# Gathered expert rows in a decoder block: arithmetic one step behind the gather, another rank and another pace in the dense pass

## The chip, the cores and the metric

The kernel runs on one core of a Trainium2 chip. The metric is device time in microseconds, the median of several runs. The engines are TensorE (PE in the profile, with its weight loads as PEld), VectorE (DVE), ScalarE (ACT), GpSimd (POOL) and SyncE (SP); each works through its own instructions in a fixed order, and waits for the others by semaphores.

## The reference, cut to what matters

One decoder block on 1024 tokens of width 1024: stick-breaking attention and a gated DeltaNet side by side, merged by gates, and then a feed-forward part that fetches single experts. All tensors are float32. The change touches the last part alone:

```python
def peer_ffn(h, w_q, keys1, keys2, u_tab, v_tab):
    q = einsum(h, w_q)                        # 8 heads, two halves of 128
    s1, s2 = q1 @ keys1.T, q2 @ keys2.T       # 128 scores each
    v1, i1 = top_k(s1, 16); v2, i2 = top_k(s2, 16)
    vals, c = top_k(v1[:, None] + v2[None], 16)
    expert = e1 * 128 + e2                    # 16384 experts
    gate = softmax(vals)
    # per block of 128 tokens, 8 heads x 16 = 128 experts for each token
    act = gelu(einsum('td,ted->te', h, u_tab[expert]))
    return einsum('te,ted->td', gate * act, v_tab[expert])
```

## The kernel before

The 1024 tokens are two halves of 512. Each half goes through the mixers (projections, attention, DeltaNet), the merge, the output projection, the norm and the routing (`half`). The feed-forward part is then done in two ways, by blocks of 128 tokens.

Blocks 2, 3, 6 and 7 are dense: every expert is computed for every token, and a gate table of zeros and gates is multiplied in. This is the dense pass (`dense`), the last stage of the program, in 128 chunks of 128 experts. In a chunk TensorE computes the scores (`scores`, 24 matmuls of 512 columns, lines 885 and 887) and the values (24 matmuls by `mm3`, lines 72 to 74), VectorE splits the loaded weights into two parts (line 64, tiles `ut` and `d_v`), multiplies the gates in (`weigh`, line 915), and computes the low part of the product after ScalarE has cast the high part (`rest`, line 906, after line 919). Every fourth chunk it adds four finished accumulators to the output (line 974). The weights stream in on SP's queue, 512 KB at a time.

Blocks 0, 1, 4 and 5 are gathered (`gather_rows`): for each of their 128 experts per token POOL fetches one row of 4 KB per token, 512 KB in all (line 1016), first from `peer_u`, then from `peer_v`. VectorE multiplies a `peer_u` row with the token's hidden state and sums it (line 1019, two instructions, the second reads the sum), or adds a `peer_v` row times its activation to the output (line 1021). That makes 4 x 256 = 1024 rows. In between, after 128 rows, the activations go through Gelu and the gates (lines 1007 and 1009), and the tile of the hidden state is replaced by the output's (line 1011); after 256 rows the output is stored (line 1025) and the next block's hidden state is loaded into the same place (line 1001).

The rows lie in the buffers `gb_row0` to `gb_row3`, used in turn; the dense pass adds two more and takes them off the list at its end. A row can be fetched only when the row that had its buffer is multiplied.

When rows are worked in is decided by `gather(phase)`, which the stages of the second half call once in each step. Each call adds `PACE[phase]` to a count of rows due, and as many whole rows are given out. The rows are given out with a number added to the scheduler's rank (`later`). The scheduler orders the instructions of each engine when the program is built; a smaller rank goes first. The row's arithmetic also gets a bond that keeps it behind VectorE's last instruction at that point (`behind`, the `anchor`). A last call without a phase gives out the rows that are left, after the dense pass.

Of the kernel before, what the change touches and what calls it, by code (L numbers as in the profile page):

```python
# [13 lines left out]
OP = mybir.AluOpType  # L14
# [13 lines left out]
CB = 256  # L28
EPS = 1e-6

PACE = dict(sb=2.2, gdn=1.5, logits=2.5, merge=2.5, out=0.5, route=0, table=0.1, dense=5.25)
NEG = -1e30
C_Q, C_K, C_V = 0, 1024, 2048
C_GQ, C_GK, C_GV, C_GZ = 3072, 4096, 5120, 6144
# [4 lines left out]
class Block:  # L39
    def __init__(self, tc, ins, out):  # L40
        self.tc, self.nc, self.i, self.out, self.tok, self.turn = tc, tc.nc, ins, out, 0, 0
        self.rows, self.due, self.delayed = None, 0.0, []


    @contextmanager
# [947 lines left out]
    def gather_rows(self, blks):  # L993

        nc = self.nc
        n = H * 16
        self.row_bufs = [(self.gp, f"gb_row{k}") for k in range(4)]
        turn = 0
        for blk in blks:
            h2 = self.gp.tile([P, D], F32, name="gb_h2", bufs=1)  # L1000
            nc.sync.dma_start(h2, self.h2_d[blk])
            act = self.gp.tile([P, n], F32, name="gb_act")
            ix = self.expert[blk]
            acc = None
            for p in range(2 * n):
                if p == n:
                    self.acts(nc.scalar.activation(act, act, AF.Gelu))
                    self.back_to_exp()
                    nc.vector.tensor_tensor(act, act, self.gate[blk], op=OP.mult)
                    acc = self.gp.tile([P, D], F32, name="gb_h2", bufs=1)  # L1010
                    nc.sync.dma_start(acc, self.x2_d[blk])
                pool, name = self.row_bufs[turn % len(self.row_bufs)]
                turn += 1
                r = pool.tile([P, D], F32, name=name, bufs=1)
                q = p % n
                nc.gpsimd.indirect_dma_start(out=r, out_offset=None, in_=self.i["peer_u" if p < n else "peer_v"][0],  # L1016
                                             in_offset=bass.IndirectOffsetOnAxis(ap=ix[:, q:q + 1], axis=0))
                if p < n:
                    i = nc.vector.scalar_tensor_tensor(r, r, 1.0, h2, op0=OP.mult, op1=OP.mult, accum_out=act[:, q:q + 1])  # L1019
                else:  # L1020
                    i = nc.vector.scalar_tensor_tensor(acc, r, act[:, q:q + 1], acc, op0=OP.mult, op1=OP.add)  # L1021
                if self.anchor is not None:
                    self.behind(i, self.anchor)
                if p == 2 * n - 1:
                    nc.sync.dma_start(self.out[0, blk * P:(blk + 1) * P, :], acc)
                yield

    def last_dve(self):
        ins = self.nc.cur_bb.bb.instructions
        return next(i for i in reversed(ins) if i.engine == mybir.EngineType.DVE)  # L1030
# [14 lines left out]
    def gather(self, phase=None):  # L1045

        if self.rows is None:
            return
        if phase is None:
            self.anchor = None  # L1050
            for _ in self.rows:
                pass
            return
        self.due += PACE[phase]
        self.anchor = self.last_dve()
        with self.later(1000000):
            while self.due >= 1:
                self.due -= 1
                next(self.rows, None)

    def half(self, half, hx, new_h, st, x2_in):

# [35 lines left out]
def block_kernel(tc, ins, out, x2_in=None, dense_blks=(2, 3, 6, 7), G=8):  # L1098
    b = Block(tc, ins, out)
    b.dense_blks = list(dense_blks)  # L1100
    nc = tc.nc
    with ExitStack() as ctx:
# [14 lines left out]
        b.pz = pool(name="pz", bufs=2, space=PSUM)  # L1117
        b.pc = pool(name="pc", bufs=2, space=PSUM)
        b.gp = pool(name="gp", bufs=1)
        gctx = ctx.enter_context(ExitStack())  # L1120
        cg = gctx.enter_context(tc.tile_pool(name="cg", bufs=1, side="right"))
        b.rb = gctx.enter_context(tc.tile_pool(name="rb", bufs=1, side="right"))
# [56 lines left out]
```

## Time and profile before

| | us |
|---|---|
| three runs, median (lowest to highest) | 3876.8 (3871.88 to 3877.51) |
| the profiled execution, its own time | 3877.26 |
| its span, first to last instruction | 3875.4 |
| TensorE busy | 3596.4 (93%) |
| VectorE busy | 3077.5 (79%) |
| ScalarE busy | 1740.7 (45%) |
| POOL busy | 1356.6 (35%) |

The span has these stages, read from the times of their lines: the first half to about 1014 us, when the first row is gathered; the second half's mixers, merge, projection, norm and routing to about 2130 us; the gate tables to about 2384 us; the dense pass to 3853 us; and the last rows to 3872 us. An engine's busy share over the whole span mixes these stages, so the views below are of single stretches.

### The profile page before, as it was taken

Reading aid. Unit: us, or ns where it says so; the run is one execution under the profiler, and the core shown is the slowest. Engines: PE = TensorE matmul, PEld = TensorE weight load, DVE = VectorE, ACT = ScalarE, POOL = GpSimd, SP = SyncE. Lnnn points to the kernel's source line nnn. Section 1 sums busy time; section 2 is a strip of 40 time slices with the busy share of each in tenths; the row PEclk is TensorE's granted clock in tenths of the full one; section 3 lists DMA queues with packets and bytes.
Section 4 is the critical chain, followed back from the end, with each engine's and each line's share of the span. In section 5 each row is a group of like instructions: output and inputs, shape, how many; then the busy total and the mean of one; then the engine's idle time right before and its main releaser. Section 6 shows DMA issues by size and latency. Waiting matters only on the chain.

```text
span 3875.4 us, 53560 instructions
## 1 busy us (share of the span) xinstructions
PE 3596.4 (93%) x18936; PEld 2983.8 (77%) x18936; DVE 3077.5 (79%) x6196; ACT 1740.7 (45%) x3846; POOL 1356.6 (35%) x1034
## 2 busy tenths in 40 slices
PE   8999999999999999998878877999999999999996
PEld 7878888788777688886667666787778787788785
DVE  5345554349988878888879998899898899899898
ACT  6755554333777655553322786222222322222221
POOL 0000000000044332223442003666666665676665
PEclk9999999999999999999989999999999999999998
DMA  4221113553377756558985568999999999999998
GB/s 121 88 82 50 55 50 115 174 186 93 96 256 265 246 191 192 191 182 290 325 307 170 158 185 289 353 361 358 334 365 358 345 371 365 348 364 374 353 359 312
DMA packets 344205, 937.49 MB, mean 242 GB/s; under 512 B 41984, under 2 KB 121088, under 8 KB 339712
## 3 DMA queue, kind: packets, MB, share of 16 engines
q0 software_dynamic: 147456, 536.94, 38.8%
q1 hardware_dynamic: 196480, 397.13, 30.1%
q8 instruction: 149, 2.44, 0.3%
q14 instruction: 120, 0.98, 0.1%
HBM read 864.22 MB, written 69.21 MB: 241 GB/s over the span
## 4 chain that ended last, share of the span: by engine, by line
PE 42%; issue 20%; POOL 12%; DVE 11%; DMA 10%; ACT 4%; SPq 0%; POOLq 0%; DVEq 0%; ACTq 0%
POOL gb_row L1016 12%; PE mm L72 6%; PE mm L74 6%; PE mm L73 6%; DMA gb_row<-peer_v,expert 5%; PE pc L848 3%; DMA gb_row<-peer_u,expert 3%; PE mm L885 2%; PE pz L532 2%; PE pz L526 2%; DVE gb_row L1019 2%; DVE w_lo L64 2%; PE mm L887 1%; PE pc L317 1%; PE pz L295 1%
## 5 line engine op out<-in xcount | busy, mean ns | idle before, releaser
L1016 POOL DMA_INDIRECT gb_row<-peer_u,expert x512 | 693.6, 1355 | 1848.2 <-DVE expert L793 1012.8
L1016 POOL DMA_INDIRECT gb_row<-peer_v,expert x512 | 661.9, 1293 | 656.4 <-DVE gb_h L1021 408.8
L1019 DVE SCALAR_TENSOR_TENSOR gb_row<-gb_row,gb_h 128x1024 f32<-128x1024 f32 x512 | 614.0, 1219 | 133.2 <-DMA gb_row<-peer_u,expert 109.7
L1021 DVE SCALAR_TENSOR_TENSOR gb_h<-gb_row,gb_act,gb_h 128x1024 f32<-128x1024 f32 x512 | 657.7, 1285 | 73.7 <-DMA gb_row<-peer_v,expert 50.4
L885 PE MATMUL mm<-hf,ut 128*128 128x512 f32 x2048 | 491.2, 391 | 6.9 <-DMA hf<-hd 6.9
L919 ACT CAST d_a<-u_act 128x512 fp32r<-128x512 f32 x128 | 79.2, 621 | 926.5 <-DVE u_act L915 917.7
L885 PEld LDWEIGHTS mm<-hf,ut 128*128 128x128 f32 x2048 | 386.1, 189 | 87.7 <-issue 7.6
L64 DVE TENSOR_TENSOR w_lo<-w_raw,w_hi 128x512 fp32r<-128x512 f32 (+1 forms) x450 | 297.6, 682 | 163.9 <-ACT w_hi L63 125.9
L63 ACT CAST w_hi<-w_raw 128x512 fp32r<-128x512 f32 (+1 forms) x450 | 262.1, 620 | 286.2 <-PE mm L73 122.6
L72 PE MATMUL mm<-h,w_hi 128*128 128x512 f32 (+1 forms) x784 | 322.9, 412 | 3.0 <-ACT pj L598 3.0
L74 PE MATMUL mm<-h,w_lo 128*128 128x512 f32 (+1 forms) x784 | 320.6, 409 | 0.0
L73 PE MATMUL mm<-h,w_hi 128*128 128x512 f32 (+1 forms) x784 | 319.7, 408 | 0.0
L72 PE MATMUL pz<-d_v,d_a 128*128 128x512 f32 x680 | 272.8, 401 | 41.2 <-DVE d_acc L974 30.1
L72 PE MATMUL mm<-w_hi,h 128*128 128x256 f32 x1024 | 299.8, 293 | 8.5 <-DVE x L647 5.7
L74 PE MATMUL mm<-w_hi,h 128*128 128x256 f32 x1024 | 294.0, 288 | 4.0 <-DVE h L64 4.0
L73 PE MATMUL mm<-w_lo,h 128*128 128x256 f32 x1024 | 295.1, 288 | 1.0 <-DVE w_lo L64 0.9
L74 PE MATMUL pz<-d_v,d_a 128*128 128x512 f32 x680 | 270.4, 398 | 0.0
L73 PE MATMUL pz<-d_v,d_a 128*128 128x512 f32 x680 | 270.4, 398 | 0.0
L887 PE MATMUL mm<-hf,ut 128*128 128x512 f32 x1024 | 257.0, 391 | 2.5 <-DVE ut L64 2.5
L887 PEld LDWEIGHTS mm<-hf,ut 128*128 128x128 f32 x1024 | 192.8, 188 | 42.8 <-DVE ut L64 3.3
L72 PEld LDWEIGHTS mm<-w_hi,h 128*128 128x128 f32 x1024 | 199.5, 195 | 16.3 <-DVE x L647 6.4
L73 PEld LDWEIGHTS mm<-w_lo,h 128*128 128x128 f32 x1024 | 199.7, 195 | 6.7 <-issue 3.8
(327 smaller groups left out, 7947.9 us busy)
## 6 DMA issues: line engine op xcount, KB each, us to landing
w_raw<-w_in SPq DMA_DIRECT2D x144, 512.0 KB
u_raw<-u_t SPq DMA_DIRECT2D x128, 512.0 KB
v_raw<-v_t SPq DMA_DIRECT2D x128, 512.0 KB
g_d<-gt_stg SPq DMA_DIRECT2D x16, 2048.0 KB
d_g<-g_d SPq DMA_DIRECT2D x31, 1024.0 KB
w_raw<-peer_w_q SPq DMA_DIRECT2D x32, 512.0 KB
gl<-pj SPq DMA_DIRECT2D x32, 256.0 KB
th<-gl SPq DMA_DIRECT2D x32, 256.0 KB
```

The costliest lines, as they stand in the source:

```text
L63: nc.scalar.copy(hi, src)
L64: nc.vector.tensor_tensor(lo, src, hi.bitcast(F32), op=OP.subtract)
L72: mm(out, l[0], r[0], start=first, stop=False)
L73: mm(out, l[0], r[1], start=False, stop=False)
L74: mm(out, l[1], r[0], start=False, stop=last)
L848: self.last_gate = mm(pg[:, u - u0], o2[:, u], o1[:, u], start=True, stop=True)
L885: mm(ps, ut[0][:, k], hx[a][:, k, x0:], start=k + a == 0, stop=False)
L887: mm(ps, ut[1][:, k], hx[0][:, k, x0:], start=False, stop=k == KD - 1)
L919: nc.scalar.copy(hi, act)
L1016: nc.gpsimd.indirect_dma_start(out=r, out_offset=None, in_=self.i["peer_u" if p < n else "peer_v"][0], in_offset=bass.IndirectOffsetOnAxis ...
L1019: i = nc.vector.scalar_tensor_tensor(r, r, 1.0, h2, op0=OP.mult, op1=OP.mult, accum_out=act[:, q:q + 1])
L1021: i = nc.vector.scalar_tensor_tensor(acc, r, act[:, q:q + 1], acc, op0=OP.mult, op1=OP.add)
```

## The change

The pace of the dense pass goes from 5.25 to 5.1 rows per call. A row's gather and its arithmetic are given out apart: `gather_rows` issues the gather and notes what is to be multiplied in a list, `landing`; the new function `multiply` gives the noted multiplications out and empties the list. Ahead of the dense pass `gather` calls `multiply` first, for the rows of the call before, and then gives out the new gathers. In the dense pass `multiply` follows each gather at once, and the rank is 800 instructions on instead of 1000000. Before the Gelu, at the end of a block, and when all buffers are in the list, `multiply` is called too. In the last call, without a phase, each gather is followed by its multiplication.

```diff
-PACE = dict(sb=2.2, gdn=1.5, logits=2.5, merge=2.5, out=0.5, route=0, table=0.1, dense=5.25)
+PACE = dict(sb=2.2, gdn=1.5, logits=2.5, merge=2.5, out=0.5, route=0, table=0.1, dense=5.1)
...
-        self.rows, self.due, self.delayed = None, 0.0, []
+        self.rows, self.due, self.delayed, self.landing = None, 0.0, [], []
...
             for p in range(2 * n):
                 if p == n:
+                    self.multiply()
                     self.acts(nc.scalar.activation(act, act, AF.Gelu))
...
-                if p < n:
-                    i = nc.vector.scalar_tensor_tensor(r, r, 1.0, h2, op0=OP.mult, op1=OP.mult, accum_out=act[:, q:q + 1])
-                else:
-                    i = nc.vector.scalar_tensor_tensor(acc, r, act[:, q:q + 1], acc, op0=OP.mult, op1=OP.add)
-                if self.anchor is not None:
-                    self.behind(i, self.anchor)
+                self.landing.append((p < n, r, h2 if p < n else acc, act[:, q:q + 1]))
                 if p == 2 * n - 1:
+                    self.multiply()
                     nc.sync.dma_start(self.out[0, blk * P:(blk + 1) * P, :], acc)
                 yield
+
+    def multiply(self):
+
+        nc = self.nc
+        for dot, r, x, a in self.landing:
+            if dot:
+                i = nc.vector.scalar_tensor_tensor(r, r, 1.0, x, op0=OP.mult, op1=OP.mult, accum_out=a)
+            else:
+                i = nc.vector.scalar_tensor_tensor(x, r, a, x, op0=OP.mult, op1=OP.add)
+            if self.anchor is not None:
+                self.behind(i, self.anchor)
+        self.landing = []
...
             self.anchor = None
             for _ in self.rows:
-                pass
+                self.multiply()
             return
         self.due += PACE[phase]
         self.anchor = self.last_dve()
-        with self.later(1000000):
+        with self.later(800 if phase == "dense" else 1000000):
+            if phase != "dense":
+                self.multiply()
             while self.due >= 1:
                 self.due -= 1
+                if len(self.landing) == len(self.row_bufs):
+                    self.multiply()
                 next(self.rows, None)
+                if phase == "dense":
+                    self.multiply()
```

Three places show what the change does to VectorE's order. Lines 1019 and 1021 of before are lines 1029 and 1031 after it. Names ending in numbers are single buffers, and their numbers shift by a few between the two programs.

The first place is VectorE in the attention of the second half, ahead of the dense pass; `sb_t`, `sb_a`, `sb_lo` are tiles of the attention. Before:

```order
L300 SCALAR_TENSOR_TENSOR sb_t<-pz_12432,sb_t 128x512
L1019 SCALAR_TENSOR_TENSOR gb_row_11745,gb_act<-gb_row_11745,gb_h_10543 128x1024
L315 TENSOR_TENSOR sb_a<-pz_12377,sb_a 128x384
L64 TENSOR_TENSOR sb_lo<-sb_t,sb_hi 128x512 x2
L1019 SCALAR_TENSOR_TENSOR gb_row_11748,gb_act<-gb_row_11748,gb_h_10543 128x1024
L315 TENSOR_TENSOR sb_a<-pz_12406,sb_a 128x512
```

And now:

```order
L300 SCALAR_TENSOR_TENSOR sb_t<-pz_12430,sb_t 128x512
L1029 SCALAR_TENSOR_TENSOR gb_row_11745,gb_act<-gb_row_11745,gb_h_10543 128x1024
L315 TENSOR_TENSOR sb_a<-pz_12374,sb_a 128x384
L64 TENSOR_TENSOR sb_lo<-sb_t,sb_hi 128x512 x2
L1029 SCALAR_TENSOR_TENSOR gb_row_11747,gb_act<-gb_row_11747,gb_h_10543 128x1024
L315 TENSOR_TENSOR sb_a<-pz_12404,sb_a 128x512
```

Nothing moved: each row's multiplication stands between the same two instructions.

The second place is VectorE in a chunk in the middle of the dense pass, while `peer_v` rows are added. Before:

```order
L1021 SCALAR_TENSOR_TENSOR gb_h_27499<-gb_row_28020,gb_act,gb_h_27499 128x1024
L1021 SCALAR_TENSOR_TENSOR gb_h_27499<-gb_row_28023,gb_act,gb_h_27499 128x1024
L64 TENSOR_TENSOR ut_28065<-u_raw,ut_28064 128x1024
L915 TENSOR_TENSOR u_act<-u_act,d_g 128x512
L1021 SCALAR_TENSOR_TENSOR gb_h_27499<-gb_row_28026,gb_act,gb_h_27499 128x1024
L906 TENSOR_TENSOR d_a_28014<-u_act,d_a_28013 128x512
L1021 SCALAR_TENSOR_TENSOR gb_h_27499<-gb_row_28029,gb_act,gb_h_27499 128x1024
```

And now:

```order
L1031 SCALAR_TENSOR_TENSOR gb_h_27643<-gb_row_28424,gb_act,gb_h_27643 128x1024
L1031 SCALAR_TENSOR_TENSOR gb_h_27643<-gb_row_28427,gb_act,gb_h_27643 128x1024
L64 TENSOR_TENSOR ut_28463<-u_raw,ut_28462 128x1024
L915 TENSOR_TENSOR u_act<-u_act,d_g 128x512
L906 TENSOR_TENSOR d_a_28412<-u_act,d_a_28411 128x512
L1031 SCALAR_TENSOR_TENSOR gb_h_27643<-gb_row_28500,gb_act,gb_h_27643 128x1024
L1031 SCALAR_TENSOR_TENSOR gb_h_27643<-gb_row_28503,gb_act,gb_h_27643 128x1024
```

The row that stood between lines 915 and 906 now stands behind line 906.

The third place is VectorE at the end of the program, from the last two adds of the dense pass on. Before:

```order
L974 TENSOR_TENSOR d_acc<-pz_33397,d_acc 128x512
L974 TENSOR_TENSOR d_acc<-pc,d_acc 128x512
L1021 SCALAR_TENSOR_TENSOR gb_h_31732<-gb_row_33474,gb_act,gb_h_31732 128x1024
L1021 SCALAR_TENSOR_TENSOR gb_h_31732<-gb_row_33477,gb_act,gb_h_31732 128x1024
...
L1021 SCALAR_TENSOR_TENSOR gb_h_31732<-gb_row_33553,gb_act,gb_h_31732 128x1024
L1021 SCALAR_TENSOR_TENSOR gb_h_31732<-gb_row_33556,gb_act,gb_h_31732 128x1024
L1176 UNCONDITIONAL_BRANCH
```

And now:

```order
L974 TENSOR_TENSOR d_acc<-pz_33340,d_acc 128x512
L974 TENSOR_TENSOR d_acc<-pc,d_acc 128x512
L1031 SCALAR_TENSOR_TENSOR gb_h_31942<-gb_row_33420,gb_act,gb_h_31942 128x1024
L1031 SCALAR_TENSOR_TENSOR gb_h_31942<-gb_row_33423,gb_act,gb_h_31942 128x1024
...
L1031 SCALAR_TENSOR_TENSOR gb_h_31942<-gb_row_33561,gb_act,gb_h_31942 128x1024
L1031 SCALAR_TENSOR_TENSOR gb_h_31942<-gb_row_33564,gb_act,gb_h_31942 128x1024
L1191 UNCONDITIONAL_BRANCH
```

Between the last add and the end stand 11 multiplications before and 29 now; 16 of the 29 are those that the last call of `gather` gives out.

## Rows read from the trace of the kernel before

**Rows 1.** Busy time of each engine in two stretches; columns in the first row.

```profile
core 0: us, PE busy (x) PEld busy (x) DVE busy (x) ACT busy (x) POOL busy (x), PEclk, DMA share, GB/s
...
2458.00:3851.00 1393.00, 1341.06 (x5802) 1100.29 (x5802) 1273.49 (x1520) 377.21 (x485) 896.75 (x643) 0.98 0.95 355
3851.00:3876.00 25.00, 0.00 (x0) 0.00 (x0) 16.31 (x15) 0.00 (x0) 7.58 (x7) 0.55 0.76 294
```

**Rows 2.** TensorE's waits in the pass: us, times, longest.

```profile
PE pz L72 <- DVE d_acc L974: 30.1, 14, 4.8
PE pc L72 <- DVE d_acc L974: 18.7, 7, 6.2
```

**Rows 3.** VectorE's waits in the pass, same view.

```profile
DVE gb_row L1019 <- DMA gb_row<-peer_u,expert: 28.5, 30, 2.3
DVE gb_h L1021 <- DMA gb_row<-peer_v,expert: 22.3, 19, 2.1
DVE d_a L906 <- ACT d_a L919: 22.0, 32, 0.7
DVE gb_row L1019 <- DMA gb_h<-h2d: 20.0, 2, 11.5
DVE gb_h L1021 <- DMA gb_h<-x2d: 15.9, 3, 7.7
```

**Rows 4.** VectorE's waits for rows ahead of the pass.

```profile
DVE gb_row L1019 <- DMA gb_row<-peer_u,expert: 65.3, 43, 4.6
DVE gb_h L1021 <- DMA gb_row<-peer_v,expert: 23.9, 21, 3.0
```

**Rows 5.** Multiplications in the pass: count, busy us, mean ns, idle before.

```profile
L1021 DVE SCALAR_TENSOR_TENSOR gb_h<-gb_row,gb_act,gb_h 128x1024 f32<-128x1024 f32 x373 | 479.9, 1287 | 44.6 <-DMA gb_row<-peer_v,expert 22.3 <-DMA gb_h<-x2d 15.9
L1019 DVE SCALAR_TENSOR_TENSOR gb_row<-gb_row,gb_h 128x1024 f32<-128x1024 f32 x271 | 322.2, 1220 | 50.7 <-DMA gb_row<-peer_u,expert 28.5 <-DMA gb_h<-h2d 20.0 <-issue 1.2
```

**Rows 6.** VectorE in order of time, one bubble: start, us, [idle before <- whom].

```profile
3197.86 0.69 DVE L906 TENSOR_TENSOR d_a<-u_act,d_a 128x512 fp32r<-128x512 f32 x1 [0.69 <-ACT d_a L919]
```

**Rows 7.** VectorE in order of time, from 3846 us to the end.

```profile
3846.43 1.29 DVE L1021 SCALAR_TENSOR_TENSOR gb_h<-gb_row,gb_act,gb_h 128x1024 f32<-128x1024 f32 x1 [0.64 <-DMA gb_row<-peer_v,expert]
3848.22 2.66 DVE L1021 SCALAR_TENSOR_TENSOR gb_h<-gb_row,gb_act,gb_h 128x1024 f32<-128x1024 f32 x2 [0.50 <-DMA gb_row<-peer_v,expert]
...
3853.20 6.66 DVE L1021 SCALAR_TENSOR_TENSOR gb_h<-gb_row,gb_act,gb_h 128x1024 f32<-128x1024 f32 x5
3861.58 1.28 DVE L1021 SCALAR_TENSOR_TENSOR gb_h<-gb_row,gb_act,gb_h 128x1024 f32<-128x1024 f32 x1 [1.72 <-DMA gb_row<-peer_v,expert]
3864.10 1.28 DVE L1021 SCALAR_TENSOR_TENSOR gb_h<-gb_row,gb_act,gb_h 128x1024 f32<-128x1024 f32 x1 [1.24 <-DMA gb_row<-peer_v,expert]
3866.61 5.24 DVE L1021 SCALAR_TENSOR_TENSOR gb_h<-gb_row,gb_act,gb_h 128x1024 f32<-128x1024 f32 x4 [1.23 <-DMA gb_row<-peer_v,expert]
```

**Rows 8.** VectorE in order of time, stage with four buffers ahead of the pass.

```profile
1253.97 1.23 DVE L1019 SCALAR_TENSOR_TENSOR gb_row<-gb_row,gb_h 128x1024 f32<-128x1024 f32 x1 [3.40 <-DMA gb_row<-peer_u,expert]
...
1260.65 1.28 DVE L1019 SCALAR_TENSOR_TENSOR gb_row<-gb_row,gb_h 128x1024 f32<-128x1024 f32 x1
...
1270.06 1.22 DVE L1019 SCALAR_TENSOR_TENSOR gb_row<-gb_row,gb_h 128x1024 f32<-128x1024 f32 x1
...
1275.34 1.22 DVE L1019 SCALAR_TENSOR_TENSOR gb_row<-gb_row,gb_h 128x1024 f32<-128x1024 f32 x1 [1.46 <-DMA gb_row<-peer_u,expert]
```

**Rows 9.** POOL in order of time, the same stage.

```profile
1255.48 1.81 POOL L1016 DMA_INDIRECT gb_row<-peer_u,expert  x1 [2.82 <-DVE gb_row L1019]
...
1270.30 1.79 POOL L1016 DMA_INDIRECT gb_row<-peer_u,expert  x1 [2.92 <-DVE gb_row L1019]
```

**Rows 10.** POOL in order of time, the last gathers.

```profile
3840.31 1.01 POOL L1016 DMA_INDIRECT gb_row<-peer_v,expert  x1 [0.30 <-issue]
...
3856.90 1.02 POOL L1016 DMA_INDIRECT gb_row<-peer_v,expert  x1 [0.30 <-issue]
```

More of the change, by code (lines that the diff above doesn't have):

```diff
@@ L996, in gather_rows @@
         n = H * 16
-        self.row_bufs = [(self.gp, f"gb_row{k}") for k in range(4)]
         turn = 0
@@ L1119, in block_kernel @@
         b.gp = pool(name="gp", bufs=1)
+        b.row_bufs = [(b.gp, f"gb_row{k}") for k in range(4)]
         gctx = ctx.enter_context(ExitStack())
```

## The prediction

> **What bounds the kernel now.** I read the stretches first, then the waits of TensorE and VectorE in the dense pass, then VectorE and POOL row by row at the end of the program and in one place ahead of the pass.
>
> [Rows 1] cut out the two stretches that count. From 2458 to 3851 us, the dense pass after its filling, TensorE is busy for 1341.06 of 1393 us, VectorE for 1273.49, and the transfer engines for 95%. From 3851 us on TensorE has nothing left. VectorE alone multiplies the last gathered rows, and the program ends when it is through.
>
> [Rows 2] are TensorE's own waits in the pass: 30.1 + 18.7 = 48.8 us, all for the adds of line 974, with which VectorE empties the accumulators. So VectorE is late there. [Rows 3] say with what. It waits 28.5 + 22.3 = 50.8 us for gathered rows, 20.0 + 15.9 = 35.9 us for the h2 and x2 tiles that change with the token block, and 22.0 us (32 times 0.69) for ScalarE's cast between lines 915 and 906. That is 108.7 of the 119.5 us in which it is idle, and no wait for the accumulators is among them: it always finds them full. The pass therefore goes at VectorE's pace, with TensorE close behind.
>
> **The change part by part.** *Ahead of the pass.* A row's multiplication is now handed to the scheduler one step after its gather. The order of VectorE's instructions, though, is the same as before from the start to the end of the gate tables; POOL's and TensorE's rows are the same to the end. The waits for gathered rows there, 65.3 + 23.9 = 89.2 us [rows 4], are waits of the same instructions in the same places. I cost this part at 0. It would bring something only if the order were not what decides, and I see no way to that. On VectorE nothing is queued differently behind a waiting row, so nothing else can become late.
>
> *In the pass.* The rank of 800 in place of 1000000 and the pace of 5.1 in place of 5.25 both show in the order. Counting rows there: behind VectorE's last add stand 29 multiplications, where 11 stood, so 18 leave the pass. And lines 915 and 906 stand next to each other 53 times, where they did 35 times; the row that stood between them now stands behind.
>
> Relief: 18 multiplications by 1.287 us (the kind that adds into the output, [rows 5]; the other kind has 1.220) are 23.2 us. Against that, 18 more bubbles by 0.69 us [rows 6] are 12.4 us. That leaves 10.8 us. The gathers in the pass fall by 18 of 644, and a buffer is used again a little later; of the 50.8 us of gather waits I let 3 go, an estimate. So the pass becomes 14 us shorter. Bounds: nothing, where TensorE, busy 96% of the time, would itself set the pace, or where the bubbles eat it up; and 48.8 us, since TensorE cannot gain more than it waits for the adds. I stay near the lower half, because 18 instructions carry only 23.2 us and the bubbles are certain.
>
> What hides the removed instructions: nothing, as long as VectorE is the late one. At the two block changes the stores and loads of lines 1025, 1001 and 900 stand in another order on SP's queue, and other instructions stand in front of the row that waits for the new h2: by my estimate 2 us more of work at the first and 4 us less at the second. With [rows 3] at 20.0 us for both waits together that is small, and the gate load now follows the second pair instead of leading it, so I set the two against each other.
>
> *After the pass.* Now 18 rows more are multiplied when TensorE, ScalarE and the weight streams have nothing left to do, so nothing hides them. They run in VectorE's order behind the 11 of before. Those took from 3853.20 to 3871.85 us, 18.65 us [rows 7]: five had their rows already, then three waited for gathers that were on the way together with the output stores.
>
> Sixteen of the rows are now also given out after the two extra buffers are gone (the list is cut back to four at the end of the pass). With four buffers, a row cannot be fetched before the row four places ahead is multiplied. One round is then: from the end of a multiplication 0.28 us until POOL starts (1253.97 + 1.23 = 1255.20, to 1255.48, in the stage with four buffers ahead of the pass, [rows 8, 9]), the time from the gather's start to its row, and the multiplication of 1.28 us. The time from start to row, with gathers and multiplications counted back from the end: the fourteenth from the end, 3840.31 to 3846.43, took 6.12 us, and the fourth, 3856.90 to 3866.61, 9.71 us beside the output stores [rows 7, 10]. Ahead of the pass, 1255.48 to 1260.65 is 5.17 and 1270.30 to 1275.34 is 5.04 us [rows 8, 9]. A round is thus 0.28 + 1.28 + 5.0 to 6.1 = 6.6 to 7.7 us for four rows. The same stage shows four rows in 6.68 us (1253.97 to 1260.65) and in 9.41 us (1260.65 to 1270.06), the second with other work between [rows 8].
>
> Of the 18 rows the first six still find buffers fetched early: 6 by 1.29 = 7.7 us. The other twelve make three rounds of 7.4 us, nearer the upper end, 22.2 us. Together 30 us. Bounds: all 18 at VectorE's own pace, 18 by 1.29 = 23.2 us; and sixteen at 9.41 / 4 = 2.35 us with two at 1.29 us, 40.2 us. I take 30, since the row at 3846.43 us, with the weight streams ended, is the nearest to the new tail.
>
> The Trainium skill, page "DMA: Bandwidth & Descriptors", section "Anatomy of one DMA — SWDGE (gpsimd) path", puts a transfer issued from GpSimd at about 2.0 us plus its bytes by 436 GB/s. For 512 KB that would be an estimate of 3.2 us, and a round of 4.8 us would be shorter than four multiplications, so the buffers would not matter and the sum would be 3886.5 us, as with the first rival below. No row here shows this: the shortest time from a gather's start to its row in the stretches above is 5.04 us.
>
> **The sum.** The profiled execution took 3877.26 us, of which 3875.4 are the span; the median of the runs is 3876.8, so its own time can stand for them. 3877.3 − 14 + 30 = 3893 us.
>
> **The rivals.**
>
> *Gathers land at once in the tail.* If VectorE's pace sets the tail, it costs 23.2 us and the end is 3877.3 − 14 + 23.2 = 3886.5 us. For it: with the streams gone the transfer engines are free. Against it: the 6.12 us from 3840.31 on, when the last weights were long on their way. Chance 0.13.
>
> *The relief pays for the tail.* The pass is saturated on the transfers (95%) and on VectorE, and gathers wait on both. Fewer rows per chunk could take away about half of the 50.8 us of gather waits: a relief of about 10.8 + 20 = 31 us, against a tail of 30, 3876 us. For it: TensorE has 48.8 us to give back, and each wait of VectorE in the pass is handed on to it. Against it: 18 rows of 644 are 3%, little to halve the waits with. Chance 0.15.
>
> *Faster.* The place is the wait for the adds of line 974. If VectorE falls below TensorE's need in most chunks, the lateness built up at a block change is worked off, and all 48.8 us go: 3877.3 − 48.8 + 30 = 3858 us. It decides from a relief of 38 us on, for then the sum is under 3869. For it: VectorE's busy time is already 68 us below TensorE's. Against it: its waits are 108.7 us, and the change does not touch the 35.9 us at the block changes. Chance 0.08.
>
> *No relief.* TensorE is the bound at 96%, the row waits stay, and the bubbles eat the rest: 3877.3 + 30 = 3907 us. Chance 0.04.
>
> That the change does not do what it says is partly the case already, ahead of the pass; it is in the forecast, and it would have to move something that the order does not show to count.
>
> **How the numbers follow.** The forecast, 3893 us, has 0.60. A measurement of this kernel tells about 0.2%, 7.8 us, from no change: faster is below 3869, slower above 3884.6 us. Slower hold the forecast, no relief, and most of the quick gathers, 0.71. Within 0.2% lie the relief that pays for the tail and the remainder of the quick gathers, 0.20. Faster is 0.09. For the range, 14 of relief may be 25, and the tail 23 to 40: from 3876, where the paying relief still is, to 3907, with no more than 2 in 10 outside. The likeliest case's own range is 3885 to 3903.
>
> **What would show it.** In the profile after: the same waits for rows ahead of the pass, near 89 us, and a start of the pass within a few us of before. The last add of line 974 near 3839 us, not 3853. Behind it 29 multiplications in some 48 us, in fours with a wait of 2 to 3 us for a gather ahead of the first. Lines 915 and 906 next to each other with 0.69 us between, some 50 times. I am wrong if the last add comes 30 us earlier or more (the relief), if the waits ahead of the pass shrink (the first part does something), or if the last 18 multiplications follow each other without waits (the tail).

## The result, and the profile after

The kernel after takes 3905.7 us (median of four runs, 3902.9 to 3909.3), the kernel before 3874.7 beside it: a ratio of 1.0080, 95% interval 1.0063 to 1.0098, 31 us slower (24 to 38). The forecast was 16 us slower, in a range that ends at 3907: the measured time lies 1.3 us inside that end, and the loss is nearly twice the one forecast. The profiled execution took 3902.92 us, with a span of 3901.2: 25.8 us more than that of before.

The same stretches as in [rows 1], and ahead of them the filling of the pass, from the end of the gate tables to the first add of line 974 (columns as in [rows 1]). The filling of before:

```profile
2374.00:2458.00 84.00, 71.79 (x322) 57.98 (x322) 59.63 (x89) 31.40 (x47) 41.63 (x30) 0.96 1.00 365
```

The filling, the pass and the end after the change:

```profile
2374.00:2465.00 91.00, 73.99 (x322) 59.50 (x322) 58.91 (x88) 32.10 (x49) 40.56 (x29) 0.94 0.95 342
2465.00:3839.00 1374.00, 1334.17 (x5802) 1095.58 (x5802) 1253.32 (x1502) 372.55 (x483) 888.54 (x625) 0.99 0.95 353
3839.00:3902.00 63.00, 0.00 (x0) 0.00 (x0) 39.88 (x34) 0.00 (x0) 32.29 (x25) 0.53 0.76 266
```

The pass is 18.5 us shorter, the end 37 us longer. The filling, which the prediction left out, is 6.8 us longer. TensorE's waits for the adds, to set against [rows 2], are down from 48.8 to 38.2 us:

```profile
PE pz L72 <- DVE d_acc L974: 28.5, 12, 5.8
PE pc L72 <- DVE d_acc L974: 9.7, 5, 3.7
```

VectorE's waits in the pass, the answer to [rows 3] (us in total, times, longest):

```profile
DVE d_a L906 <- ACT d_a L919: 33.0, 48, 0.7
DVE gb_row L1029 <- DMA gb_row<-peer_u,expert: 24.8, 23, 2.5
DVE gb_row L1029 <- DMA gb_h<-h2d: 18.9, 2, 10.6
DVE gb_h L1031 <- DMA gb_row<-peer_v,expert: 16.9, 11, 3.0
DVE gb_h L1031 <- DMA gb_h<-x2d: 12.4, 3, 5.6
```

The bubbles (the waits of line 906 for ScalarE's cast) cost 11.0 us more, the gathered rows 9.1 less, the block changes 4.6 less; VectorE's busy time fell by 20.2 us. Ahead of the pass the waits for rows are much as in [rows 4], 94.5 us where 89.2 were:

```profile
DVE gb_row L1029 <- DMA gb_row<-peer_u,expert: 70.8, 37, 6.2
DVE gb_h L1031 <- DMA gb_row<-peer_v,expert: 23.7, 21, 3.7
```

VectorE from the last adds on, the answer to [rows 7] (start, duration, count, and in brackets the wait ahead):

```profile
3841.05 0.68 DVE L974 TENSOR_TENSOR d_acc<-pc,d_acc 128x512 f32<-128x512 f32 x1
3841.65 6.55 DVE L1031 SCALAR_TENSOR_TENSOR gb_h<-gb_row,gb_act,gb_h 128x1024 f32<-128x1024 f32 x5
...
3853.85 6.57 DVE L1031 SCALAR_TENSOR_TENSOR gb_h<-gb_row,gb_act,gb_h 128x1024 f32<-128x1024 f32 x5 [0.42 <-DMA gb_row<-peer_v,expert]
3866.00 5.25 DVE L1031 SCALAR_TENSOR_TENSOR gb_h<-gb_row,gb_act,gb_h 128x1024 f32<-128x1024 f32 x4 [5.58 <-DMA gb_row<-peer_v,expert]
3872.74 1.28 DVE L1031 SCALAR_TENSOR_TENSOR gb_h<-gb_row,gb_act,gb_h 128x1024 f32<-128x1024 f32 x1 [1.49 <-DMA gb_row<-peer_v,expert]
...
3884.94 2.67 DVE L1031 SCALAR_TENSOR_TENSOR gb_h<-gb_row,gb_act,gb_h 128x1024 f32<-128x1024 f32 x2 [1.67 <-DMA gb_row<-peer_v,expert]
3888.16 1.28 DVE L1031 SCALAR_TENSOR_TENSOR gb_h<-gb_row,gb_act,gb_h 128x1024 f32<-128x1024 f32 x1 [0.54 <-DMA gb_row<-peer_v,expert]
...
3896.32 1.28 DVE L1031 SCALAR_TENSOR_TENSOR gb_h<-gb_row,gb_act,gb_h 128x1024 f32<-128x1024 f32 x1 [0.98 <-DMA gb_row<-peer_v,expert]
```

The 29 rows take from 3841.65 to 3897.60, 55.95 us; 18.65 + 30 = 48.65 were expected. For the last twelve a round of four takes (3888.16 − 3872.74) / 2 = 7.7 us, and the last one 8.16; 7.4 were forecast. But no wait of 2 to 3 us stands ahead of each four, as was expected: most rows wait by themselves, 0.3 to 1.7 us. What was not forecast is the wait of 5.58 us at 3866.00. POOL's gathers around it, the answer to [rows 10]:

```profile
3855.41 1.86 POOL L1016 DMA_INDIRECT gb_row<-peer_v,expert  x1 [3.00 <-DVE gb_h L1031]
3857.57 1.02 POOL L1016 DMA_INDIRECT gb_row<-peer_v,expert  x1 [0.30 <-issue]
3859.37 1.86 POOL L1016 DMA_INDIRECT gb_row<-peer_v,expert  x1 [0.78 <-DVE gb_h L1031]
```

A gather starts at 3855.41, 10.6 us ahead of the row that waits, but by the numbers of the buffers it is not that row's. VectorE's next multiplication there takes the gather of 3859.37, the third; the first two stand behind it. This gather's row comes 6.6 us after its start. POOL could not start it earlier. Its row is the first one given out after the list of buffers is cut from six to four. By the numbers it gets the buffer of the row multiplied last but one, and the 0.78 us that POOL waits at 3859.37 are for that multiplication.

So I put the order of VectorE's multiplications beside the order of POOL's gathers in the whole program, by the buffers' numbers. Of 1024 multiplications 33 stand at another place than their gather in before, 50 in after; 23 and 34 of these stand in the filling and just behind it, and 3 in the tail of after. In the filling, multiplications 353 to 370 take these gathers (both counted from 0, the gathers along POOL):

```
before 355 356 357 343 359 347 360 358 363 365 361 362 364 366 367 368 369 370
after  357 343 344 358 359 355 360 363 356 366 361 367 362 368 364 370 365 374
```

In after a row that was fetched early is multiplied every second time, and the next one is hardly on its way: 361, 367, 362, 368. The rank is a likely cause, to be tested: with 800 the rows of the pass go ahead of those given out before it, which still have 1000000. VectorE waits for rows in the filling 20.1 us in before and 28.6 us in after (one line of the waits of each):

```profile
DVE gb_row L1019 <- DMA gb_row<-peer_u,expert: 20.1, 12, 5.1
```

```profile
DVE gb_row L1029 <- DMA gb_row<-peer_u,expert: 28.6, 13, 6.6
```

This gave two theories for the 25.8 us: the pace makes all of it (pass and tail), or the rank has a share of its own by the order of rows. And for the tail: four buffers and a gather's way, the transfers beside the output stores, or the order.

### The profile page after: what moved, and what is told of

Its sections match the earlier page's. It is cut to its first block, busy times and chain, and to the rows that moved or that the text cites. A ratio compares the mean times of both kernels' runs of the same rounds, so it can differ in the third digit from the quotient of the medians.

```text
span 3901.2 us, 53527 instructions
## 1 busy us (share of the span) xinstructions
PE 3589.0 (92%) x18936; PEld 2978.7 (76%) x18936; DVE 3079.6 (79%) x6196; ACT 1735.5 (44%) x3846; POOL 1372.6 (35%) x1034
## 4 chain that ended last, share of the span: by engine, by line
PE 36%; issue 25%; POOL 14%; DMA 10%; DVE 10%; ACT 4%; SPq 0%; POOLq 0%; DVEq 0%; ACTq 0%
POOL gb_row L1016 14%; PE mm L72 6%; PE mm L74 6%; PE mm L73 6%; DMA gb_row<-peer_v,expert 5%; PE pc L848 3%; DMA gb_row<-peer_u,expert 2%; PE pz L532 2%; PE pz L526 2%; DVE w_lo L64 1%; DVE gb_row L1029 1%; DVE gb_h L1031 1%; PE pz L522 1%; PE pc L317 1%; PE pz L295 1%
## 5 line engine op out<-in xcount | busy, mean ns | idle before, releaser
L1016 POOL DMA_INDIRECT gb_row<-peer_u,expert x512 | 707.5, 1382 | 1850.8 <-DVE expert L793 1008.9
L72 PEld LDWEIGHTS mm<-w_hi,h 128*128 128x128 f32 x1024 | 200.4, 196 | 18.9 <-DVE x L647 6.9
L74 PEld LDWEIGHTS mm<-w_hi,h 128*128 128x128 f32 x1024 | 200.3, 196 | 7.0 <-DVE h L64 5.2
```

What stands on the lines that cost most here:

```text
L72: mm(out, l[0], r[0], start=first, stop=False)
L74: mm(out, l[1], r[0], start=False, stop=last)
```

## The experiments

Stages of the profiled executions in us, read from starts and ends of lines: *ahead* to the end of the gate tables (line 829), *filling* to the first add of line 974, *pass* to the first of its last four adds, *tail* to the end. So *ahead* ends at 2374 us in before, earlier than the 2384 named for the gate tables above. The last column is the ratio of times to those of before, run beside each kernel, with its 95% interval.

| kernel | ahead | filling | pass | tail | ratio |
|---|---|---|---|---|---|
| before | 2374.1 | 84.3 | 1392.4 | 24.6 | 1 |
| after | 2374.3 | 91.1 | 1373.9 | 61.9 | 1.0080 (1.0063 to 1.0098) |
| pace alone | 2369.3 | 86.6 | 1372.6 | 62.0 | 1.0040 (1.0026 to 1.0055) |
| rank undone | 2381.4 | 84.4 | 1378.9 | 61.7 | 1.0053 (1.0039 to 1.0067) |
| pace undone | 2371.6 | 89.7 | 1401.1 | 24.1 | 1.0043 (1.0027 to 1.0060) |
| pace undone, again | 2375.6 | 90.3 | 1400.0 | 24.0 | 1.0031 (1.0019 to 1.0044) |
| after, in order | 2366.6 | 85.8 | 1378.2 | 60.6 | 1.0056 (1.0038 to 1.0074) |
| before, in order | 2375.0 | 86.4 | 1388.8 | 24.4 | 1.0012 (1.0002 to 1.0022) |
| after, six buffers | 2375.3 | 90.7 | 1378.8 | 57.4 | 1.0076 (1.0060 to 1.0092) |
| after, no dense stores | 2373.5 | 90.9 | 1374.0 | 58.6 | 1.0051 (1.0038 to 1.0064) |
| after, in order, six | 2367.4 | 85.7 | 1378.1 | 50.4 | 1.0029 (1.0017 to 1.0040) |
| before, pace 5.35 | 2372.3 | 83.8 | 1408.1 | 8.6 | 1.0011 (1.0001 to 1.0020) |
| before, rest first | 2374.2 | 78.5 | 1355.6 | 31.0 | 0.9915 (0.9900 to 0.9931) |
| rest first, pace 5.4 | 2372.3 | 78.6 | 1411.1 | 8.3 | 0.9970 (0.9959 to 0.9981) |

The column *ahead* tells how far single executions scatter: after and rank undone have the same instructions in the same order there, down to the rows, and lie 7 us apart; before and pace alone, too, and lie 5 us apart. So a stage is compared over several kernels.

**The pace alone**, in the kernel before.

```diff
-... dense=5.25)
+... dense=5.1)
```

> The kernel before with the dense pace at 5.1 and nothing else. 29 rows stand after the last add, 53 times lines 915 and 906 stand next to each other, as in the kernel after. Pace theory: the whole loss, +25 to +34 us, ratio 1.0065 to 1.009; pass 18 us shorter, tail 37 us longer. Rival (rank and filling carry 7 us of the loss): +18 to +24 us, ratio 1.005 to 1.006, with the first add near 2458 us.

Measured 3893.0 us, 16 us slower: below both ranges, nearer the rival's, and the first add came at 2455.9. All of the pass's gain and all of the tail's loss is here: its pass (1372.6 us) and its tail (62.0) are as long as those of after; the filling is not. VectorE's waits in this pass:

```profile
DVE d_a L906 <- ACT d_a L919: 34.4, 50, 0.7
DVE gb_row L1019 <- DMA gb_row<-peer_u,expert: 20.2, 23, 2.6
DVE gb_row L1019 <- DMA gb_h<-h2d: 19.4, 2, 10.4
DVE gb_h L1021 <- DMA gb_h<-x2d: 16.7, 3, 6.5
DVE gb_h L1021 <- DMA gb_row<-peer_v,expert: 16.2, 18, 2.4
```

Here the gathered rows cost 36.4 us, 14.4 less than in before, and the block changes 36.1, as in before: the 4.6 us that these lost in after do not come from the pace.

**The pace undone**, in the kernel after.

```diff
-... dense=5.1)
+... dense=5.25)
```

> The kernel after with the dense pace put back to 5.25; handing out one step behind and rank 800 stay. VectorE's order then differs from that of before in 52 rows, all in the first 40 chunks of the pass, and 11 rows stand after the last add, as before. Pace theory (the loss is the 18 rows left for the tail): the time of before, ratio 0.998 to 1.002, tail from the last adds to the end near 21 us, waits for rows ahead of the pass near 89 us. Rival (the rank of 800, which moves rows in the filling of the pass, costs the 6.9 us by which the first add came later after the change): first add near 2465 us, ratio 1.0015 to 1.002. Rival (handing out one step behind gains or loses something ahead of the pass): the start of the pass moves by more than 7 us either way.

Measured 3892.6 us, 17 us slower with the tail and the pace of before. The pace theory falls: what is left of the change costs by itself. It also costs more than the rival on the rank allowed (1.0043 where 1.0015 to 1.002 were expected), and the first add came at 2461.3.

**The rank undone**, in the kernel after.

```diff
-        with self.later(800 if phase == "dense" else 1000000):
+        with self.later(1000000):
```

> The kernel after with the rank put back to 1000000; one step behind and the pace of 5.1 stay. Rank theory (the rank makes the rows of the pass overtake on POOL those given out before it, so that VectorE multiplies them in another order than they are fetched in, and buffers lie full; 7 to 11 us in the filling): row waits between 2370 and 2520 us back from 35 to 27 us, first add near 2456 us, the time of the pace alone, ratio 1.003 to 1.0055. Rival (one step behind costs it): first add near 2465 us, ratio 1.0065 to 1.0085.

By kinds of instructions its order is that of the pace alone on all engines. By the rows, 30 gathers and 30 multiplications ahead of the gate tables' end stand at other places; behind it none does, so there it is a second measurement of the pace alone. Ratio 1.0053, in the range of the rank theory; the filling is 84.4 us, and the row waits between 2370 and 2520 us are 20.2 us, where after has 31.1. The first add came at 2465.7 all the same, because this execution was 7 us late already at the gate tables. Handing out one step behind is thus no part of the loss in the filling: with it, and without the rank, the filling is that of before. Ahead of the gate tables' end it reorders those 30 rows; whether that costs a few us there, the scatter of *ahead* does not let one see.

**In order, in the kernel after.** Each gather gets a bond to the gather before it, each multiplication to the one before it (`g` is the gather, `i` the multiplication).

```diff
+                if self.last_g is not None:
+                    self.behind(g, self.last_g.ins)
+                self.last_g = g
...
+            if self.last_m is not None:
+                self.behind(i, self.last_m.ins)
+            self.last_m = i
```

> The kernel after with two rules for the scheduler: a gather stands behind the gather before it on POOL, a multiplication behind the multiplication before it on VectorE. The rank of 800 and the pace of 5.1 stay; 56 bubbles, 29 rows after the last add. Of 50 rows that stood at another place than their gather none is left. Theory (the order of rows against gathers is what the rank costs): first add 2452 to 2458 us, row waits between 2370 and 2520 us 20 to 27 us, ratio 1.003 to 1.0045. Rival (rows rank earlier, so they displace the weight splits that TensorE waits for in the filling): first add near 2465 us, ratio 1.007 to 1.008.

The rank stays and the filling is back at 85.8 us; the waits for rows in it are 15.9 us:

```profile
DVE gb_row L1033 <- DMA gb_row<-peer_u,expert: 15.9, 10, 5.6
```

The ratio, 1.0056, misses the expected range by a little, with an interval that reaches into it. Of the 10 us by which this profiled execution is shorter than that of after, 7.7 lie ahead, 5.3 in the filling and 1.3 in the tail, and the pass is 4.3 longer; so the time alone does not show the filling's part. That the order of rows against gathers makes the filling long is shown by the stage: 89.7 to 91.1 us in the five executions with the rank and without the bond, 83.8 to 86.6 in the seven without the rank or with the bond (rest first left out, whose filling differs otherwise).

The tail hardly changed, 60.6 us. With the rows in order the wait is still there, at the same place:

```profile
3851.37 1.86 POOL L1017 DMA_INDIRECT gb_row<-peer_v,expert  x1 [7.91 <-DVE gb_h L1035]
```

```profile
3856.69 1.28 DVE L1035 SCALAR_TENSOR_TENSOR gb_h<-gb_row,gb_act,gb_h 128x1024 f32<-128x1024 f32 x1 [4.27 <-DMA gb_row<-peer_v,expert]
```

POOL stands idle until the buffer of the row multiplied last but one is free, and VectorE then waits 4.27 us. So the order alone does not make the long wait in the tail.

**In order, in the kernel before.** The same bonds, pace 5.25.

> The kernel before with the same two rules, pace 5.25. In before 33 rows stand at another place than their gather, two of them 11 and 13 places late, which hold their buffers for 54 us; here none. Theory: some of the 27.3 us of row waits between 2370 and 2520 us go, 3 to 8 us; ratio 0.998 to 0.9993, first add near 2452 us. Rival (the buffers held in the filling of before cost nothing, since other rows are ready): no change, 0.9995 to 1.0005. Rival (in order, VectorE's queue stands behind the oldest row where a younger one was there): 3 to 6 us slower, 1.001 to 1.0015.

Ratio 1.0012: no gain. That is the second rival's number, and its interval reaches the first rival's. The few rows that before multiplies late cost it nothing that the order could give back.

**The pace undone, again**, to see where the rank's cost lies.

> The kernel after with the dense pace back at 5.25, a second time: what rank 800 costs, of which the profiles of seven kernels show 4 to 7 us in the filling (90 us with it and rows out of order, 84 to 86 us without) and the medians 10 to 23 us. Theory (all of it lies in the filling): filling 89 to 91 us, pass 1389 to 1395 us as before, ratio 1.001 to 1.002. Rival (it goes on into the pass): filling 89 to 91 us, pass 1399 to 1403 us again, ratio 1.003 to 1.005.

Filling 90.3, pass 1400.0 us, 3887.0 us: the rival. At a pace of 5.25 the rank costs 5 to 6 us in the filling and 8 us more in the pass, 3.9 and 5.5 of them (in its two executions) before the second group of adds:

```profile
2375.00:2466.00 91.00, 73.40 (x322) 59.00 (x322) 59.60 (x89) 31.07 (x49) 40.87 (x30) 0.94 0.95 339
2466.00:3866.00 1400.00, 1346.44 (x5802) 1104.95 (x5802) 1274.71 (x1520) 377.57 (x485) 905.75 (x645) 0.98 0.95 354
```

At 5.1 the pass shows no such cost (1373.9 with the rank, 1372.6 and 1378.9 without).

**Six buffers for the tail**, in the kernel after. The list is not cut, and the last rows are given out while the two extra buffers still exist.

```diff
-            del self.row_bufs[4:]
             for n, blk in enumerate(blks):
                 nc.sync.dma_start(self.out[0, blk * P:(blk + 1) * P, :], acc[:, n])
+            self.gather()
```

> The kernel after, in which the rows after the pass keep all six buffers (the list is not cut back to four). Orders of the pass unchanged. Buffer theory (rounds of four, 7.2 to 8.2 us, set the tail): with six a round of about 7 us holds six rows, which VectorE takes at 1.28 us each, so the tail is set by VectorE or POOL: 29 rows by 1.29 to 1.65 us, 38 to 48 us where 56 were; 8 to 18 us less than the kernel after, ratio to before 1.003 to 1.006. Rival (the transfers themselves are slow at the end, 184 to 270 GB/s in parts of the tail): the wait of 5.6 us and the tail of 53 to 57 us stay, ratio 1.007 to 1.008.

The time is the rival's. The tail is between: from the last add's end 51.5 us, and 57.4 as a stage, where after has 61.9. But the reason is not the rival's:

```profile
3873.77 9.21 DVE L1031 SCALAR_TENSOR_TENSOR gb_h<-gb_row,gb_act,gb_h 128x1024 f32<-128x1024 f32 x7 [8.18 <-DMA gb_row<-peer_v,expert]
```

Here VectorE multiplies the sixth of six gathers first. Behind the wait all rows follow with 0.41 us of wait or less, as the buffer theory has it; the wait of 8.18 us ate what they gained.

**No dense stores**, in the kernel after: the four stores of `acc` are left out, and with them the dense part of the output.

> The kernel after without the four stores of the dense part of the output (that part of the output is left out; the rows of the other part are all computed and stored). Theory of the transfers (2.1 MB of stores take the transfer engines from the gathers at the head of the tail): the gathers there come 5 to 6 us earlier, the wait of 5.6 us shrinks to 1 to 3, the tail from the last add to the end is 5 to 8 us shorter, ratio 1.0055 to 1.0065. Rival (four buffers and the latency of a gather set the tail by themselves): the wait of 5 to 6 us stays, the tail is 0 to 2 us shorter, ratio 1.0075 to 1.008.

The tail is 3.3 us shorter, between the two theories, and the wait at the third gather is still 4.43 us:

```profile
3862.04 5.25 DVE L1029 SCALAR_TENSOR_TENSOR gb_h<-gb_row,gb_act,gb_h 128x1024 f32<-128x1024 f32 x4 [4.43 <-DMA gb_row<-peer_v,expert]
```

The stores cost the tail some 3 us; they are not the main part of that wait. The ratio, 1.0051, is a little below the first theory's range and 11 us below that of after; the stages of the two profiled executions show 4 us of it, and where the rest lies was not seen.

**In order and six buffers**, in the kernel after.

> The kernel after with gathers and multiplications each in the order they are given out, and with all six buffers kept for the rows behind the pass. With six buffers alone the tail fell only from 61.9 to 57.4 us, since VectorE there waited 8.18 us for a gather that POOL starts five places later than its multiplication stands; in order without more buffers it was 60.6 us. Theory (buffers and order each hide the other's gain): a round of six takes VectorE 7.7 us and a gather's way 5.5 us, so the tail falls to 46 to 51 us from the last group of adds to the end, ratio to before 1.002 to 1.004. Rival (POOL, 1.3 to 2.2 us per gather, or the transfers set the tail): 55 to 58 us, ratio 1.005 or more.

```profile
3846.59 9.24 DVE L1035 SCALAR_TENSOR_TENSOR gb_h<-gb_row,gb_act,gb_h 128x1024 f32<-128x1024 f32 x7 [0.65 <-DMA gb_row<-peer_v,expert]
3856.28 2.71 DVE L1035 SCALAR_TENSOR_TENSOR gb_h<-gb_row,gb_act,gb_h 128x1024 f32<-128x1024 f32 x2 [0.45 <-DMA gb_row<-peer_v,expert]
```

The tail is 50.4 us, 11.5 less than in after, where order alone brought 1.3 and buffers alone 4.5; no wait in it is longer than 1.7 us. Ratio 1.0029, as expected. Order and buffers hid each other's gain: with the order alone the cut of the list delays the next row's gather (the 7.91 us above), and with the buffers alone a late gather's row is multiplied first (the 8.18 us).

**The other way: pace 5.35**, in the kernel before.

> The kernel before with the dense pace at 5.35 and nothing else: no row stands after the last add, and 23 times lines 915 and 906 stand next to each other instead of 35. By the slope of the change (18 rows fewer made the pass 18.5 us shorter) 11 rows more make the pass 11 us longer; the tail falls from 18.7 us to about 3: 4 to 5 us less than before, ratio 0.998 to 0.999. Rival (in the pass a row costs only its instruction less the bubble it fills, 0.6 us): 8 to 9 us less, ratio 0.9975. Rival (the pass is saturated and each further row costs its full time and a wait, 2 us): 6 us more, ratio 1.0015.

Missed, and no gain: 1.0011, nearest the second rival. The tail is 16 us shorter, the pass 15.7 us longer, 1.4 us for each of 11 rows: the slope of the change, 1.0, did not hold here.

**Rest first**, in the kernel before. The 32 bubbles cost 22.0 us [rows 3]; the call that makes line 906 is moved.

```diff
+                rest()
                 a3 = act.rearrange("p (c t) -> p c t", t=GT)
                 nc.vector.tensor_tensor(a3, a3, gts[e1 // GQ][:, :, e1 % GQ], op=OP.mult)
...
                 nc.scalar.copy(hi, act)
-                rest()
```

> The kernel before, pace 5.25 and rank 1000000, with one call moved: the subtraction of line 906 for the chunk ahead stands before the multiplication of line 915, not behind it. In VectorE's order lines 915 and 906 then stand next to each other 2 times instead of 35, and 15 rows stand after the last add instead of 11. Theory (the bubbles of 0.69 us are paid in full by the pass, VectorE being the late engine): 33 by 0.69 = 22.8 us out of the pass and 4 rows by 1.0 us, tail 4 rows by 2.1 us longer: 18 us less than before, ratio 0.995 to 0.997. Rival (the bubbles are slack, since gathers would be waited for instead): no change or the 4 us of the longer tail, 0.9995 to 1.0015.

3841.1 us, 33 us less than before: more than expected. Its pass, and VectorE's waits in it:

```profile
2453.00:3808.00 1355.00, 1331.91 (x5823) 1097.45 (x5821) 1266.65 (x1520) 375.75 (x485) 911.35 (x642) 0.99 0.96 365
```

```profile
DVE gb_row L1019 <- DMA gb_row<-peer_u,expert: 29.3, 32, 3.1
DVE gb_h L1021 <- DMA gb_row<-peer_v,expert: 17.2, 15, 2.2
DVE gb_h L1021 <- DMA gb_h<-x2d: 17.1, 3, 8.1
DVE gb_row L1019 <- DMA gb_h<-h2d: 13.9, 2, 7.9
...
DVE d_a L906 <- ACT d_a L920: 1.4, 2, 0.7
```

The bubbles are down from 22.0 to 1.4 us, the waits for gathered rows from 50.8 to 46.5. TensorE's waits for the adds fell from 48.8 to 18.1 us:

```profile
PE pz L72 <- DVE d_acc L974: 14.8, 6, 5.1
...
PE pc L72 <- DVE d_acc L974: 3.3, 2, 2.9
```

So the pass gained more (36.8 us) than the bubbles had (20.6), with 642 gathers in it where 643 were, and TensorE busy 1332 of 1355 us. VectorE's rows show most of the rest: 4.9 us less at the block changes, 4.3 less for gathered rows, and 6.8 less busy time (1266.65 where 1273.49 was). Why these fell with the bubbles was not tested.

**Rest first with pace 5.4.**

> The same move of line 906 with the dense pace at 5.4: no row after the last add. Against the kernel with the move alone: pass 15 rows by 1.0 us longer, tail 18 to 20 us shorter. Theory as there: 20 to 25 us less than before, ratio 0.994 to 0.995. Rival (bubbles are slack): 0.9985 to 1.0005.

Both missed: 0.9970. The tail went as expected, but the pass took 1411.1 us, 55 us more for 15 rows and longer than that of before, and the row waits rose from 46.5 to 78.4 us:

```profile
DVE gb_row L1019 <- DMA gb_row<-peer_u,expert: 45.1, 38, 2.6
DVE gb_h L1021 <- DMA gb_row<-peer_v,expert: 33.3, 28, 2.4
```

Why the waits rise so steeply between the two paces stays open; rest first with a lower pace, or with the rows in order, was not tried. Of all kernels here rest first at 5.25 is the quickest.

## Why the prediction was right in sign and short in size

*Ahead of the pass, 0:* nothing shows otherwise. The stage is 2374.3 us against 2374.1, the row waits 94.5 against 89.2. The reason given holds for the kinds of instructions only: by the rows, 30 gathers and multiplications there changed places, and a cost of a few us would not be seen in the scatter.

*The pass, −14:* 18.5 us in the profile, 13.5 to 20 in the seven kernels at 5.1. VectorE's busy time fell by 20.2 us (23.2 forecast), the bubbles took 11.0 (12.4 forecast). In this pair the mis-sized terms were the gather waits, 9.1 us where I let 3 go, and the block changes, 4.6 us where I set the two against each other; with the pace alone only the first was (14.4 us). Four of the seven kernels lie within 1 us of the forecast.

*The tail, +30:* 37.3 us by its rows, inside its bounds (23.2 to 40.2) but 7 above the value taken. The rounds of four were sized well: 23.6 us for twelve rows from 3872.74 to 3896.32, 22.2 forecast. The step that failed is "the first six still find buffers fetched early: 6 by 1.29". There the wait of 5.58 us lies, so that these six end after 14.9 us (from about 3859.1 to 3874.02) instead of 7.7. Two things make it, and either is enough. The cut of the list gives the first row after it a buffer that is still in use: with the order mended the wait is 4.27 us. And VectorE holds two rows that were fetched before it: with six buffers, and the order not mended, a wait of 8.18 us stands there. With both mended no wait is longer than 1.7 us, and the tail is 50.4 us.

*What had no term:* the filling. This is a second step that failed: the rank got no price ahead of the last add. The start of the pass was to come within a few us of before; it came 6.9 us later. "POOL's and TensorE's rows are the same to the end" was read with the buffers' numbers left out; the kinds of rows are the same, which row they fetch is not. The rank was counted only by what it leaves behind the last add, and that is nothing: 29 rows and 53 bubbles come from the pace alone. What it does is in the filling, 6.8 us in this pair, 5.2 between the means of the two groups of kernels.

The sum by stages: 0.2 + 6.8 − 18.5 + 37.3 = 25.8 us, the difference of the profiled executions; 16 was forecast. The errors are 6.8 for the filling, 7.3 in the tail and, the other way, 4.5 in the pass. That the time still fell inside the range is in part luck: its upper end is the time of the case without relief, and nothing in it stood for a longer filling. By the ratios the pace makes 16 us alone and 21 together with one step behind, and the rank with one step behind 12 and 17 us at 5.25. The profiles give the rank 11 to 15 us at that pace, and 4.5 to 6.7 in the filling at 5.1. Where the rest of the 31 us lies in the other executions of after was not seen; its profiled execution was the quickest of four.

*The rivals.* "Gathers land at once in the tail" (3886.5 us) fell: the row at 3872.74 came 5.18 us after its gather's start at 3867.56, with the transfer engines idle when it started. The Trainium skill, page "DMA: Bandwidth & Descriptors", section "Anatomy of one DMA — SWDGE (gpsimd) path", would give an estimate of 3.2 us for 512 KB; no run here shows so short a way: the shortest in any trace here is 4.4 us, ahead of the pass in rank undone. "The relief pays for the tail" and "Faster" would have needed 30 and 38 us of relief; the change gave 18.5. That such a relief exists is shown by rest first, which took 36.8 us out of the pass by another way. "No relief" (3907 us) is nearest in time, and wrong in its reason: the relief was there, and the filling and the tail's order took it back.

## What to carry to other kernels

In the pass a row cost about its duration of 1.29 us: 1.0 us each for the 18 taken out, 1.4 each for 11 put in (in rest first 3.7 each between the two paces). Behind the pass a row cost 2.1 us (37.3 by 18), since a round of four buffers, 7.7 us, held one gather's way. Even with six buffers and the rows in order 18 rows made the tail 25.8 us longer and the pass 14.3 shorter, so moving them to the end did not pay here. Where a scheduler orders two engines apart, compare the order of the loads with the order of their uses by buffer number, not by kind of instruction: a use that stands ahead of its turn waits for a late load and keeps early loads in their buffers. A short wait that returns in many chunks of the late engine (0.69 us, 32 times) can be worth more than the rows one moves to relieve it.

## What was not expected of the chip

A gather's instruction on POOL is not of one length. In the kernel after 473 of the 1024 take less than 1.1 us and 252 take 1.7 us or more. The long ones are more frequent where POOL had just waited, but a wait does not decide it: at 3855.41 one took 1.86 us behind a wait of 3.00 us, at 3874.30 another 0.94 behind 0.99. What decides it stays open.

Taking 20.6 us of short waits out of VectorE shortened the pass by 36.8 us, while at a higher pace all of it was lost again (1355.6 against 1411.1 us). And two kernels with the same instructions in the same order reached the same line 7 us apart (2374.3 and 2381.4 us), so that a stage's difference of a few us needs several profiles.
